# Building gate one-hots from bf16 comparisons of eight tokens, with most lookups on VectorE

## The chip, the cores and the metric

The kernel runs on one core of a Trainium2 chip. The metric is the device time of one execution in microseconds (us). Engines are named as in the profile: PE is TensorE's matmul, PEld its weight load, DVE VectorE, ACT ScalarE, POOL GpSimd, SP SyncE, which issues most transfers. SBUF is the memory on the core, PSUM the accumulators behind PE.

## The reference

One layer of an encoder for 1024 tokens of width 1024. The first half mixes tokens (a causal convolution beside an RWKV-7 recurrence). The second half, PEER, is where the change lies: each token picks, for each of 8 heads, 16 of 128 x 128 = 16384 experts by two lists of 128 keys.

```python
v1, i1 = lax.top_k(s1, PEER_TOPK)          # 16 best of 128 first keys, per head
v2, i2 = lax.top_k(s2, PEER_TOPK)          # 16 best of 128 second keys
cand = (v1[..., :, None] + v2[..., None, :]).reshape(..., 256)
sc, ci = lax.top_k(cand, PEER_TOPK)        # 16 best sums
experts = (jnp.take_along_axis(i1, ci // 16, -1) * 128
           + jnp.take_along_axis(i2, ci % 16, -1))
gates = jax.nn.softmax(sc, axis=-1)
...
z = einsum('td,tkd->tk', h, peer_u[experts])
y2 = einsum('tk,tkd->td', gelu(z) * gates, peer_v[experts])
```

Inputs and output are float32.

## The kernel before

The 1024 tokens are eight tiles of 128. Tiles 0 to 4 (`DT`) are computed densely: all 16384 experts are applied to them, each multiplied by a gate that is zero for experts that weren't picked. Tiles 5 to 7 (`GT`) gather their experts' rows by indirect DMA. The program has these stages:

- Up to about 1000 us: the input projection and the recurrence (chunks of 64 tokens). Between its matmuls run, as fill work, `front` (output projection, norms) and `query` (query projection, scores, top 16 of the keys) of token pairs 0 to 255, 256 to 511 and, later, 512 to 767.
- Then, without the recurrence: `front(768)`, `query(512)`, `query(768)`, with lookups (`choose`) stepped every `TSLOW` and gate matrices (`gate_matrix`) every `TGATE` steps, the latter at a higher priority for the planner. The planner orders the instructions of each engine by a simulated timeline; on the chip each engine then runs its list in order and waits on semaphores.
- From 1404 us: the dense loop over 32 groups of 4 x 128 experts, with the gathers of tiles 5 to 7 on POOL (indirect DMA) and DVE beside it.

`choose` handles one tile's lookups: top 16 of the 72 candidate sums (`best16`), then the position in each key list, then the key itself. That last step ("the lookup") is done for four heads in one pass, two passes for each of the two key lists: compare a small iota with the position (line 968, DVE, a one-hot `oh` in bf16), multiply by the keys (line 971), and sum over the 16 places. Line 971 and the sum run on the engine `E`: POOL for tiles 0 to 3, DVE for tiles 4 and 5 (`V if t0 >= LV`). On POOL the sum is a tree of additions that halve the one-hot (lines 977, 979); on DVE it is one reduction (line 974). The rows of keys and gates go to DRAM (`sel_d`); tiles 6 and 7 do the whole of it later, inside the dense loop, two heads at a time.

`gate_matrix` turns one dense tile's keys and gates into a 128 x 128 matrix per token, first key by second key. Keys and gates are loaded back and transposed by PE into PSUM (`selbank`; for tile 0 into a `mgate` bank), so that a column is a token. Then, for each four tokens (a group; 32 groups a tile, 160 in all): DVE compares the iota with the first keys into `oa` (line 1028) and with the second keys of three tokens into `ob` (line 1032); POOL multiplies these three by the gates (line 1034); ACT makes the fourth token's column from a square and a clamp (lines 1037, 1038); PE multiplies `ob` by `oa`, four matmuls in float32 (line 1040); ACT copies the product to `stage` (line 1041). Every 32 tokens a stage of 2 MB is written to `G_d` from ACT's queue (line 1048). The dense loop reads it back as `gmat`.

The tiles `oa` and `ob` have three buffers each, `stage` two and a third at times. Pages (`page`, a ring of `NPAGE` buffers of 2 KB) hold most of the other working tiles; `ident` and `iota` are constants.

Of the kernel before, what the change touches and what calls it, by code (L numbers as in the profile page):

```python
# [61 lines left out]
LV = 512  # L62
# [4 lines left out]
NPAGE = 31  # L67
# [3 lines left out]
GB = 3  # L71
# [14 lines left out]
def layer_kernel(ctx, tc, x, cols, c_row, cond_w, w_in, w2a2, g2, w_out, ln_rows, wq, keys, peer_u, peer_ut, peer_v, peer_vt, out):  # L86
# [17 lines left out]
    iota = const.tile([128, 128], F32)  # L104
    G.iota(iota, pattern=[[1, 128]], base=0, channel_multiplier=0, allow_small_or_imprecise_dtypes=True)
# [21 lines left out]
    sel_d = dt([3, 128, 128], "sel_d", 8)  # L127
    score_d = {t: [dram.tile([128, 512], F32, name=f"score_d{t}_{g}") for g in range(4)] for t in range(6, 8)}
# [23 lines left out]
    iota_q = const.tile([128, TOPK, TOPK], BF, name="iota_q")  # L152
    V.tensor_copy(iota_q, iota[:, :TOPK, None].to_broadcast([128, TOPK, TOPK]))
# [763 lines left out]
    def choose(tt, val, idx, h0, nh, nb, new, E):  # L917
# [21 lines left out]

        place = pos.bitcast(I32)  # L940
# [19 lines left out]
        put = lambda w, t: None if tt == DT[-1] else ld(sel_d[tt][w][:, h0 * TOPK:h0 * TOPK + n], t.rearrange("p h r -> p (h r)"))  # L960
        for half, sel in ((0, isel), (1, jsel)):
            ib = qb[:, 2 + half]
            A.activation(ib, idx[:, :, half, :], AF.Copy)
            for hh in range(0, nh, nb):
# [8 lines left out]
                if E is V:  # L973
                    V.tensor_reduce(fo[half][:, hs], oh.rearrange("p h q r -> p h r q"), axis=AX.X, op=OP.add)  # L974
                    continue
# [19 lines left out]
    def gate_matrix(tt, chosen):  # L995

        three = lambda nm: gb[0].tile([128, 3, 128], F32, name=nm)
        quad_ = lambda nm: gb[0].tile([128, 4, 128], F32, name=nm, bufs=GB)
        st = three("selt")
        if chosen:  # L1000
            s = [t.rearrange("p h r -> p (h r)") for t in chosen]
        else:
            kept_ = three("selr")
            s = [kept_[:, w] for w in range(3)]
            for w in range(3):
                ld(s[w], sel_d[tt][w])

        selbank.append(selbank.pop(0))
        pt = (selbank[0].tile([128, 512], F32, tag="mgate", name="selbank", bufs=1) if selbank[0] else mgate())[:, :384]
        pt = pt.rearrange("p (w t) -> p w t", w=3)  # L1010
        for w in range(3):
            T.transpose(pt[:, w], s[w], ident)
        A.activation(st, pt, AF.Copy)
        i1, i2, gt = (st[:, w] for w in range(3))
        if selbank[0]:
            i1, i2 = pt[:, 0], pt[:, 1]
        neg = three("selneg")
        A.activation(neg, pt, AF.Copy, scale=-1.0)
        for r0 in range(0, 128, TB):
# [5 lines left out]
            for q in range(0, TB, 4):  # L1025
                ts = slice(r0 + q, r0 + q + 4)
                oa, ob = quad_("oa"), quad_("ob")
# [344 lines left out]
```

## Time and profile before

| | |
|---|---|
| Time, median of 3 runs | 3225.45 us (3225.2 to 3225.85) |
| The profiled execution's own time | 3225.41 us, span 3223.5 us |
| PE busy | 2995.2 us (93%) |
| PEld busy | 2582.2 us (80%) |
| DVE busy | 2563.2 us (80%) |
| POOL busy | 1796.7 us (56%) |
| ACT busy | 1198.1 us (37%) |
| DMA | 922.30 MB, mean 286 GB/s |
| Mean granted TensorE clock | 0.953 |

Shares of the whole span are averages over stages with different limits, so the tables below give busy time by stretch. A row such as "L1028 DVE TENSOR_TENSOR oa<-iota,selbank" names the line in the kernel, the engine, the operation, and output and inputs by their tiles; buffer numbers are left out. "Idle before" is the time for which the engine waited ahead of the instruction, with what ended the wait.

### The profile page before, as it was taken

What the parts mean: (1) busy time and instruction counts of PE and PEld (TensorE: products, weight loads), DVE (VectorE), ACT (ScalarE), POOL (GpSimd) and SP (SyncE); (2) the same over time, 40 slices, a digit from 0 to 9 for tenths busy, and PEclk for the clock granted to TensorE, in tenths of its full rate; (3) what the DMA queues carried; (4) which work ended last, traced back from release to release, by engine and by line L of the source; (5) the groups of instructions that cost most, each with busy time, mean ns of one, the idle gap of its engine ahead of it and who ended that gap; (6) DMA issues with size and microseconds to landing.
All of it is one profiled execution on the core that took longest, in us unless ns stands there. A gap on an engine that the chain in (4) does not pass through costs nothing.

```text
span 3223.5 us, 53860 instructions
## 1 busy us (share of the span) xinstructions
PE 2995.2 (93%) x19952; PEld 2582.2 (80%) x19952; DVE 2563.2 (80%) x5612; ACT 1198.1 (37%) x2314; POOL 1796.7 (56%) x1408
## 2 busy tenths in 40 slices
PE   6968999899799589899999999999999999999995
PEld 4735677478688479899899988899989898999994
DVE  6279566856977979958999999898878777778788
ACT  5562344253353467552223232322323232222222
POOL 2410011133441853367777776787878777787872
PEclk9979899979699799999999999999999999999997
DMA  8876465378566898999999989899999999999994
GB/s 307 290 208 229 135 179 170 113 235 288 169 193 240 266 307 253 311 350 329 340 336 328 341 317 321 307 336 347 339 335 339 346 328 354 329 345 330 344 339 171
DMA packets 411782, 922.30 MB, mean 286 GB/s; under 512 B 81744, under 2 KB 221568, under 8 KB 389504
## 3 DMA queue, kind: packets, MB, share of 16 engines
q1 hardware_dynamic: 218688, 474.23, 43.2%
q0 software_dynamic: 110592, 402.70, 33.8%
q10 hardware_dynamic: 82240, 41.94, 4.6%
q8 instruction: 156, 2.56, 0.3%
q14 instruction: 106, 0.87, 0.1%
HBM read 788.91 MB, written 129.85 MB: 285 GB/s over the span
## 4 chain that ended last, share of the span: by engine, by line
PE 46%; DVE 13%; DMA 3%; issue 2%; ACT 1%; POOL 1%; SPq 0%; ACTq 0%; DVEq 0%; POOLq 0%
PE mg L1268 22%; PE md L1302 21%; DVE grow L1194 2%; PE mgate L1040 2%; DVE yacc L1307 1%; DVE gy L1201 1%; DMA vraw<-peer_vt 1%; PE mm L194 1%; DMA G_d<-stage 1%; DVE oa L1028 1%; DVE ob L1032 1%; DMA grow<-peer_v,eid 0%; DVE tkg L974 0%; DVE oh L968 0%; DVE bnst L202 0%
## 5 line engine op out<-in xcount | busy, mean ns | idle before, releaser
L1268 PE MATMUL mg<-h2h,uhi 128*128 128x320 f32 x2024 | 626.1, 309 | 8.0 <-DVE al L1274 8.0
L1268 PE MATMUL mg<-h2l,uhi 128*128 128x320 f32 x2024 | 625.1, 309 | 0.0
L1268 PE MATMUL mg<-h2h,ulo 128*128 128x320 f32 x2024 | 624.9, 309 | 0.0
L1201 DVE SCALAR_TENSOR_TENSOR gy<-grow,gz,gy 128x1024 f32<-128x1024 f32 x381 | 487.7, 1280 | 19.1 <-DMA grow<-peer_v,eid 17.3
L1302 PE MATMUL md<-vhi,al 128*128 128x512 f32 x1280 | 497.9, 390 | 0.0
L1302 PE MATMUL md<-vlo,ah 128*128 128x512 f32 x1280 | 496.5, 390 | 0.0
L1302 PE MATMUL md<-vhi,ah 128*128 128x512 f32 x1280 | 491.7, 391 | 4.1 <-DVE yacc L1307 2.1
L1194 DVE SCALAR_TENSOR_TENSOR grow<-grow,gh 128x1024 f32<-128x1024 f32 x384 | 460.6, 1210 | 25.6 <-DMA grow<-peer_u,eid 24.2
L1186 POOL DMA_INDIRECT grow<-peer_u,eid x384 | 363.1, 946 | 187.3 <-DVE grow L1194 78.4
L1186 POOL DMA_INDIRECT grow<-peer_v,eid x384 | 361.9, 942 | 187.6 <-DVE gy L1201 99.4
L1268 PEld LDWEIGHTS mg<-h2h,uhi 128*128 128x128 f32 x2024 | 379.9, 188 | 16.8 <-DVE al L1274 11.5
L1268 PEld LDWEIGHTS mg<-h2l,uhi 128*128 128x128 f32 x2024 | 379.9, 188 | 4.6
L1268 PEld LDWEIGHTS mg<-h2h,ulo 128*128 128x128 f32 x2024 | 379.9, 188 | 3.2
L1229 POOL TENSOR_TENSOR vlo<-vraw,vhi 128x1024 fp32r<-128x1024 f32 x128 | 309.0, 2414 | 32.4 <-ACT vhi L1227 30.0
L1229 POOL TENSOR_TENSOR ulo<-uraw,uhi 128x1024 fp32r<-128x1024 f32 x128 | 309.1, 2415 | 29.9 <-ACT uhi L1227 27.9
L1307 DVE TENSOR_TENSOR yacc<-md,yacc 128x512 f32<-128x512 f32 x310 | 210.6, 685 | 124.9 <-PE md L1302 124.3
L1302 PEld LDWEIGHTS md<-vhi,ah 128*128 128x128 f32 x1280 | 239.6, 188 | 53.1 <-ACT ah L1273 4.0
L1034 POOL TENSOR_TENSOR ob<-ob,selt 128x384 f32<-128x384 f32 x160 | 144.9, 907 | 241.7 <-DVE ob L1032 163.4
L1302 PEld LDWEIGHTS md<-vlo,ah 128*128 128x128 f32 x1280 | 240.3, 188 | 48.6
L1227 ACT ACTIVATE vhi<-vraw 128x1024 fp32r<-128x1024 f32 x128 | 135.2, 1056 | 387.8 <-DMA vraw<-peer_vt 369.9
L1302 PEld LDWEIGHTS md<-vhi,al 128*128 128x128 f32 x1280 | 240.3, 188 | 45.1 <-DVE al L1274 0.2
L182 POOL TENSOR_TENSOR wsplit<-wraw,wsplit 128x1024 fp32r<-128x1024 f32 x46 | 112.6, 2450 | 221.0 <-ACT wsplit L181 214.3
(404 smaller groups left out, 5916.8 us busy)
## 6 DMA issues: line engine op xcount, KB each, us to landing
uraw<-peer_ut SPq DMA_DIRECT2D x128, 512.0 KB, 7.1
vraw<-peer_vt SPq DMA_DIRECT2D x128, 512.0 KB, 5.5
wsplit<-split_wq SPq DMA_DIRECT2D x48, 1024.0 KB, 6.7
G_d<-stage ACTq DMA_DIRECT2D x20, 2048.0 KB, 13.6
gmat<-G_d SPq DMA_DIRECT2D x32, 1024.0 KB, 8.1
cw<-cond_w SPq DMA_DIRECT2D x48, 512.0 KB, 5.0
wsplit<-split_w_out SPq DMA_DIRECT2D x24, 1024.0 KB, 5.9
split_w_in<-wsplit SPq DMA_DIRECT2D x22, 1024.0 KB, 5.1
```

What stands on the lines that cost most here:

```text
L182: G.tensor_sub(lo, raw, hi.bitcast(F32))
L194: T.matmul(pt, l[:, k, :], r[k], start=i == 0, stop=i == 3 * KD - 1)
L1034: G.tensor_mul(ob[:, :3], ob[:, :3], gt[:, ts.start:ts.start + 3, None].to_broadcast([128, 3, 128]))
L1040: T.matmul(pt[:, t, :], ob[:, t, :], oa[:, t, :], start=True, stop=True)
L1186: G.indirect_dma_start(out=r, out_offset=None, in_=peer_u if k < 128 else peer_v, in_offset=bass.IndirectOffsetOnAxis(ap=eid[:, k % 128:k ...
L1194: V.scalar_tensor_tensor(r, r, 1.0, ht, op0=OP.mult, op1=OP.mult, accum_out=z[:, i:i + 1])
L1201: V.scalar_tensor_tensor(y, r, z[:, i - 128:i - 127], y, op0=OP.mult, op1=OP.add)
L1227: A.activation(hi, raw, AF.Copy)
L1229: G.tensor_sub(lo, raw, hi.bitcast(F32))
L1268: T.matmul(p, l[:, k, :], r[k][:, bs], start=i == 0, stop=i == 3 * KD - 1)
L1302: T.matmul(p, l[:, ts], r[:, e % 2, :], start=e == 0 and q == 0, stop=e == 3 and q == 2)
L1307: ins = V.tensor_add(ya, p, ya)
```

## The change

Gate one-hots: the keys of dense tiles are kept in bf16 (exact, since they are below 128) and transposed as bf16. For eight tokens at a time DVE compares a wide bf16 iota (`iota_e`, each value eight times) with the keys, once for each key list, into bf16 masks laid out key by token, three buffers. For each four tokens ACT copies the first mask to `oa` in float32, POOL multiplies three tokens of the second mask by the gates into `ob`, and DVE multiplies the fourth. The square and the clamp on ACT and the negated copy (`selneg`) are gone. `oa` has two buffers now, `ob` three.

Row loads: two transfers (bf16 keys from the new `keyb_d`, gates from `sel_d`) into a buffer of `ob`, in place of three into a buffer of their own.

Lookups: `LV` goes from 512 to 256, so that tiles 2 and 3 run line 971 and the sum on DVE; only the first pair (tiles 0 and 1) stays on POOL. Wherever all eight heads are done at once (tiles 0 to 5) the sum is the tree of additions, on either engine; the reduction stays for tiles 6 and 7.

Memory: `NPAGE` goes from 31 to 30. `iota` is no longer a constant: it is made once at the start for `iota_q`, and again in a page when the gate buffers are opened.

```diff
-LV = 512
+LV = 256
-NPAGE = 31
+NPAGE = 30
-GB = 3
+GB = 2, 3
+MB = 3
...
+    keyb_d = [dram.tile([2, 128, 128], BF, name=f"keyb_d{i}") for i in range(8)]
...
# choose
+        dense = tt in DT
...
+        if dense:
+            fo = qb[:, 4], qb[:, 5]
+        put = lambda w, t: None if tt == DT[-1] else ld((keyb_d if dense and w < 2 else sel_d)[tt][w][...], ...)
...
-                if E is V:
+                if nh < NH:
                     V.tensor_reduce(fo[half][:, hs], oh.rearrange("p h q r -> p h r q"), axis=AX.X, op=OP.add)
                     continue
                 for w in (8, 4, 2):
...
# gate_matrix
+            got = quad_("ob", GB[1]).rearrange("p t e -> p (t e)")
+            kb = got.bitcast(BF)[:, 0:256].rearrange("p (w k) -> p w k", w=2)
+            sg = got[:, 128:256]
+            ld(kb, keyb_d[tt].rearrange("w p k -> p w k"))
+            ld(sg, sel_d[tt][2])
...
-        for w in range(3):
-            T.transpose(pt[:, w], s[w], ident)
-        A.activation(st, pt, AF.Copy)
-        neg = three("selneg")
-        A.activation(neg, pt, AF.Copy, scale=-1.0)
+        keys_ = pt.bitcast(BF)[:, 0:256].rearrange("p (w k) -> p w k", w=2)
+        for w, k in enumerate((k1, k2)):
+            T.transpose(keys_[:, w], k, identb)
+        T.transpose(pt[:, 128:256], sg, ident)
+        gt = gb[0].tile([128, 128], F32, name="selt")
+        A.activation(gt, pt[:, 128:256], AF.Copy)
+        gv = pt[:, 128:256] if selbank[0] else gt
+        if not selbank[0]:
+            both = gb[0].tile([128, 2, 128], BF, name="selk2")
+            A.activation(both, keys_, AF.Copy)
+            keys_ = both
...
-                V.tensor_tensor(oa, iota[:, None, :].to_broadcast([128, 4, 128]),
-                                i1[:, ts, None].to_broadcast([128, 4, 128]), op=OP.is_equal)
-                V.tensor_tensor(ob[:, :3], iota[:, None, :].to_broadcast([128, 3, 128]),
-                                i2[:, ts.start:ts.start + 3, None].to_broadcast([128, 3, 128]), op=OP.is_equal)
-                G.tensor_mul(ob[:, :3], ob[:, :3], gt[:, ts.start:ts.start + 3, None].to_broadcast([128, 3, 128]))
-                A.activation(o, iota, AF.Square, bias=neg[:, 1, c])
-                A.activation(o, o, AF.Relu, bias=gt[:, c], scale=neg[:, 2, c])
+                if q % 8 == 0:
+                    masks = []
+                    for w in range(2):
+                        m = gb[0].tile([128, 128, 8], BF, name="mask", bufs=MB)
+                        V.tensor_tensor(m, iota_e, keys_[:, w, None, r0 + q:r0 + q + 8].to_broadcast([128, 128, 8]),
+                                        op=OP.is_equal)
+                        masks.append(m)
+                ma, mb = (m[:, :, q % 8:q % 8 + 4].rearrange("p e t -> p t e") for m in masks)
+                oa, ob = quad_("oa", GB[0]), quad_("ob", GB[1])
+                A.activation(oa, ma, AF.Copy)
+                c = r0 + q
+                G.tensor_mul(ob[:, :3], mb[:, :3], gt[:, c:c + 3, None].to_broadcast([128, 3, 128]))
+                V.tensor_mul(ob[:, 3], mb[:, 3], gv[:, c + 3:c + 4].to_broadcast([128, 128]))
```

More of the change, by code (lines that the diff above doesn't have):

```diff
@@ L152, in layer_kernel @@
     iota_q = const.tile([128, TOPK, TOPK], BF, name="iota_q")
+    iota = fe.tile([128, 128], F32, name="iota")
+    G.iota(iota, pattern=[[1, 128]], base=0, channel_multiplier=0, allow_small_or_imprecise_dtypes=True)
     V.tensor_copy(iota_q, iota[:, :TOPK, None].to_broadcast([128, TOPK, TOPK]))
@@ L959, in choose @@
         yield
-        put = lambda w, t: None if tt == DT[-1] else ld(sel_d[tt][w][:, h0 * TOPK:h0 * TOPK + n], t.rearrange("p h r -> p (h r)"))
+        if dense:
+            fo = qb[:, 4], qb[:, 5]
+        put = lambda w, t: None if tt == DT[-1] else ld((keyb_d if dense and w < 2 else sel_d)[tt][w][:, h0 * TOPK:h0 * TOPK + n],
+                                                        t.rearrange("p h r -> p (h r)"))
         for half, sel in ((0, isel), (1, jsel)):
@@ L995, in gate_matrix @@
     def gate_matrix(tt, chosen):
[L997 to L999 removed]
+        iota_e, identb = gb[1:]
+        quad_ = lambda nm, bufs: gb[0].tile([128, 4, 128], F32, name=nm, bufs=bufs)
         if chosen:
[L1001 removed]
+            k1, k2, sg = [t.rearrange("p h r -> p (h r)") for t in chosen]
         else:
[L1003 to L1018 removed]
+            got = quad_("ob", GB[1]).rearrange("p t e -> p (t e)")
+            kb = got.bitcast(BF)[:, 0:256].rearrange("p (w k) -> p w k", w=2)
+            sg = got[:, 128:256]
+            k1, k2 = kb[:, 0], kb[:, 1]
+            ld(kb, keyb_d[tt].rearrange("w p k -> p w k"))
+            ld(sg, sel_d[tt][2])
+        selbank.append(selbank.pop(0))
+        pt = selbank[0].tile([128, 512], F32, tag="mgate", name="selbank", bufs=1) if selbank[0] else mgate()
+        keys_ = pt.bitcast(BF)[:, 0:256].rearrange("p (w k) -> p w k", w=2)
[9 more added lines that the diff above has]
+            keys_ = both
         for r0 in range(0, 128, TB):
@@ L1067, in layer_kernel @@
             gb.append(fex.enter_context(tc.tile_pool(name="gb", bufs=1)))
+            iota = page("iota", w=128)
+            G.iota(iota, pattern=[[1, 128]], base=0, channel_multiplier=0, allow_small_or_imprecise_dtypes=True)
+            iota_e = gb[0].tile([128, 128, 8], BF, name="iota_e")
+            V.tensor_copy(iota_e, iota[:, :, None].to_broadcast([128, 128, 8]))
+            identb = gb[0].tile([128, 128], BF, name="identb")
+            V.tensor_copy(identb, ident)
+            gb.extend((iota_e, identb))
         if c < 14:
```

5 lines of the change are left out of this document (removed).

## The prediction

> **What bounds the kernel now.** I first read the busy time by stretch, cutting the span where the limiting engine changes. Each row gives length, then busy us and instruction count of PE, PEld, DVE, ACT and POOL, then granted clock, DMA share and GB/s.
>
> ```profile
> 860.00:1000.00 140.00, 131.91 (x1571) 117.89 (x1569) 117.11 (x342) 74.36 (x177) 57.83 (x59) 0.91 0.55 179
> ...
> 1055.00:1130.00 75.00, 43.08 (x201) 36.06 (x200) 72.47 (x174) 34.53 (x70) 66.31 (x66) 0.75 0.80 258
> 1130.00:1202.00 72.00, 56.50 (x421) 53.17 (x419) 58.01 (x163) 46.08 (x113) 37.98 (x39) 0.94 0.95 314
> 1202.00:1260.00 58.00, 57.71 (x481) 57.65 (x482) 50.42 (x222) 40.09 (x98) 19.25 (x24) 0.96 0.94 293
> 1260.00:1367.00 107.00, 92.27 (x751) 88.87 (x749) 106.59 (x318) 69.96 (x170) 40.24 (x40) 0.97 0.85 277
> 1367.00:1404.00 37.00, 34.90 (x264) 33.88 (x265) 21.49 (x39) 28.02 (x65) 18.86 (x22) 0.95 1.01 343
> 1404.00:3223.00 1819.00, 1771.31 (x9930) 1611.57 (x9928) 1516.71 (x2684) 516.23 (x848) 1342.92 (x1024) 0.99 0.91 328
> ```
>
> Gate matrices are built from 860 to 1404 us. After that comes the dense expert loop (1819 us, PE 1771 of them), which contains no changed line. So whatever the change is worth, it is worth it before 1404 us. Between 1055 and 1130 DVE is full (72.47 of 75) and PE half empty; the same from 1260 to 1367 (DVE 106.59 of 107, PE 92.27). From 1202 to 1260 and from 1367 on PE is full instead, and from 1130 to 1202 the DMA share is 0.95. The chain of waits, asked for each of those five stretches in turn, says the same:
>
> ```profile
> by line: DVE oa L1028 10.0%; DVE cand L932 9.0%; DVE ob L1032 8.2%; DVE oh L968 7.9%; DVE xt L837 7.1%; DVE rstd L212 5.1%; DVE bnst L202 4.8%; PE mm L819 4.0%; ACT xn L220 3.9%; DVE nbias L218 3.6%; issue 3.1%; DVE tkf L941 2.5%; DVE xt L8
> ...
> by line: DMA G_d<-stage 39.6%; DMA wsplit<-split_wq 12.7%; DMA selr<-sel_d 12.4%; DMA keys<-keys 7.2%; PE mgate L1040 5.5%; DVE xt L837 3.5%; ACT ob L1038 2.5%; ACT xt L220 2.0%; ACT stage L1041 1.7%; SPq L830 1.7%; DVE oa L1028 1.7%; SPq L
> ...
> by line: PE mm L194 52.3%; PE mgate L1040 38.7%; PE mm L891 8.5%; ACT ob L1038 0.9%; issue 0.1%
> ...
> by line: DVE oa L1028 13.6%; DVE tkg L974 12.2%; DVE ob L1032 11.5%; issue 8.7%; DVE oh L971 8.1%; DVE oh L968 5.5%; ACT stage L1041 3.8%; ACT ob L1037 2.7%; DVE h2lo L232 2.7%; DVE cand L781 2.3%; ACT ob L1038 2.1%; DVE tku L780 2.1%; DVE
> ...
> by line: PE mgate L1040 53.3%; PE md L1268 19.2%; PE mm L194 7.7%; PE mm L891 4.8%; ACT L1270 3.5%; PE mg L1268 2.8%; POOL ob L1034 2.3%; ACT stage L1041 2.1%; ACT ob L1038 2.1%; ACT ob L1037 1.9%; issue 1.3%; ACT md L1270 1.2%
> ```
>
> Look at the first item of each: DVE, DMA (the write of a finished gate block), PE, DVE, PE. A cheaper DVE instruction shortens the first and the fourth stretch only; in the others it is hidden by what their line names.
>
> **Gate one-hots.** The next fence is the view of the tiles oa, ob and stage: min/median/max ns of each instruction.
>
> ```profile
> L1028 DVE TENSOR_TENSOR oa<-iota,selbank x128: 630/675/690, 1003.8 to 1399.1; 128x512 f32<-128x512 f32 x128
> L1028 DVE TENSOR_TENSOR oa<-iota,selt x32: 647/693/2415, 864.1 to 994.1; 128x512 f32<-128x512 f32 x32
> ...
> L1037 ACT ACTIVATE ob<-iota,selneg x160: 383/393/444, 860.2 to 1400.3; 128x128 f32<-128x128 f32 x160
> L1038 ACT ACTIVATE ob<-ob,selt,selneg x160: 478/493/537, 861.1 to 1401.5; 128x128 f32<-128x128 f32 x160
> L1034 POOL TENSOR_TENSOR ob<-ob,selt x160: 818/827/2817, 867.4 to 1400.4; 128x384 f32<-128x384 f32 x160
> L1032 DVE TENSOR_TENSOR ob<-iota,selbank x128: 535/544/552, 1004.4 to 1399.7; 128x384 f32<-128x384 f32 x128
> ...
> L1041 ACT ACTIVATE stage<-mgate x160: 572/597/634, 875.9 to 1403.1; 128x512 f32<-128x512 f32 x160
> ...
> L977 POOL TENSOR_TENSOR oh<-oh x48: 420/868/1683, 835.2 to 1128.3; 128x512 bf16<-128x512 bf16 x16, 128x256 bf16<-128x256 bf16 x16, 128x128 bf16<-128x128 bf16 x16
> L968 DVE TENSOR_TENSOR oh<-iota_q,tkb x24: 677/684/2400, 824.1 to 1347.6; 128x1024 bf16<-128x1024 bf16 x24
> L971 POOL TENSOR_TENSOR oh<-oh,tkb x16: 1904/2214/4514, 824.9 to 1099.4; 128x1024 bf16<-128x1024 bf16 x16
> L979 POOL TENSOR_TENSOR tkg<-oh x16: 299/303/615, 845.8 to 1130.3; 128x64 f32<-128x64 bf16 x16
> L971 DVE TENSOR_TENSOR oh<-oh,tkb x8: 1209/1212/1843, 1308.6 to 1353.3; 128x1024 bf16<-128x1024 bf16 x8
> ...
> L968 DVE TENSOR_TENSOR loh<-iota_q,ltkb x16: 404/416/1252, 1540.9 to 2141.6; 128x512 bf16<-128x512 bf16 x16
> L971 DVE TENSOR_TENSOR loh<-loh,ltkb x16: 673/680/2301, 1541.8 to 2143.0; 128x512 bf16<-128x512 bf16 x16
> ...
> L983 DVE TENSOR_TENSOR tkg<-tkg,mx x6: 277/282/406, 819.5 to 1336.7; 128x128 f32<-128x128 f32 x6
> ```
>
> Now, per four tokens: DVE 0.675 + 0.544 = 1.219 us; ACT 0.393 + 0.493 for the fourth column and 0.597 for the stage copy, 1.48 us; POOL 0.827 us. After: half of two bf16 comparisons of 1024 elements each, that is one per four tokens. L968 is the same operation on the same size and type, with the iota laid out and a run of neighbours as the other operand: 0.684 us. Its small form (0.416 for 512) against L971 on DVE (0.680 for 512, 1.212 for 1024, where one operand stands still in the innermost dimension) shows that this form takes about half a nanosecond an element and the other a whole one. Here the innermost dimension is eight neighbouring tokens on both sides, as in L968. The one thing no row shows is a bf16 operand that lies in PSUM. Bounds: 0.684 (L968) and 1.212 (L971 on DVE). I take 0.684, since layout and type are those of L968, and L1028 costs no more from PSUM (0.675) than from SBUF (0.693).
>
> The Trainium skill does not agree with itself on this. Its page "VectorE: DVE Perf Modes", section "The perf-mode tier table", puts a two-tensor operation with any PSUM operand at one element a cycle; the section "Why PSUM operands drop a tier" on the same page allows the two-element mode for 16-bit data there. By the first the mask would cost as L971 does, and the time is that of the first rival below; by the second the sum stands. No run here shows a 16-bit PSUM operand yet.
>
> The fourth column on DVE is 128 elements; the nearest row is L983 (0.282). So DVE per four tokens: 0.684 + 0.282 = 0.966, a saving of 0.25 us. ACT swaps 0.886 us for one copy of 512 elements, bounded by the stage copy (0.597) and by the 0.886 it replaces; I take 0.6, so ACT falls to 1.2 us. It is no limit in any of the stretches (at most 70 of 107 us). POOL's product keeps its 384 elements: 0.827. The four matmuls keep their shapes. New waits: a mask (three buffers) waits for the ACT copies and POOL products of the pair before, and the fourth column for the matmuls three groups back; behind them on DVE stand the top-16 searches and lookups, and PE waits for those only through later tiles. Their likeness today is L1028's wait for the matmuls, 1.4 us in the first stretch and 0.2 us in the fourth (below); I take the same again.
>
> **Lookups.** DVE rows of 1055 to 1130, then POOL's; below them, for comparison, one DVE row of 1130 to 1202 and three of 1260 to 1367 (count | busy us, mean ns of one):
>
> ```profile
> L1028 DVE TENSOR_TENSOR oa<-iota,selbank 128x512 f32<-128x512 f32 x17 | 11.4, 670 | 1.4 <-PE mgate L1040 1.4
> L968 DVE TENSOR_TENSOR oh<-iota_q,tkb 128x1024 bf16<-128x1024 bf16 x6 | 10.6, 1827 | 0.0
> ...
> L932 DVE TENSOR_TENSOR cand<-vi 128x64 f32<-128x64 f32 (+2 forms) x8 | 7.1, 920 | 0.0
> L837 DVE TENSOR_TENSOR xt<-xt,row_g 128x512 f32<-128x512 f32 x4 | 5.9, 1530 | 0.0
> ...
> L218 DVE SCALAR_TENSOR_TENSOR nbias<-bnmv,rstd 128x1 f32<-128x1 f32 x4 | 4.2, 1062 | 0.0
> L212 DVE TENSOR_TENSOR rstd<-rstd,rnew 128x1 f32<-128x1 f32 x4 | 4.0, 1029 | 0.0
> ...
> L977 POOL TENSOR_TENSOR oh<-oh 128x512 bf16<-128x512 bf16 (+2 forms) x24 | 18.4, 788 | 0.0
> L971 POOL TENSOR_TENSOR oh<-oh,tkb 128x1024 bf16<-128x1024 bf16 x7 | 15.4, 2225 | 2.7 <-DVE oh L968 2.7
> ...
> L212 DVE TENSOR_TENSOR rstd<-rstd,rnew 128x1 f32<-128x1 f32 x4 | 0.5, 153 | 0.0
> ...
> L1028 DVE TENSOR_TENSOR oa<-iota,selbank 128x512 f32<-128x512 f32 x40 | 26.9, 672 | 0.3 <-PE mgate L1040 0.2
> ...
> L974 DVE TENSOR_REDUCE tkg<-oh 128x64 f32<-128x1024 bf16 x8 | 15.9, 2032 | 0.0
> ...
> L932 DVE TENSOR_TENSOR cand<-vi 128x64 f32<-128x64 f32 (+2 forms) x12 | 2.2, 218 | 0.0
> ```
>
> Tiles 2 and 3 (the second pair) move from POOL to DVE, and seven of their eight passes lie in the first stretch. Each took POOL 2.2 + 3 x 0.79 + 0.30 = 4.9 us. On DVE a pass is the product, 1.212 (L971 DVE), and four bf16 additions of 512, 256, 128 and 64 elements. The first is 0.416 (the 512 form of L968); 1024 against 512 gives 0.52 ns an element and 0.15 us fixed, so 0.28, 0.21 and 0.18 follow, together 1.1 us. That adds 8 x 2.3 = 18.5 us to DVE. Against it stands what POOL does to DVE in this stretch: L968 means 1.83 us where its median is 0.684, L932 0.92 where it is 0.218 later, L218 and L212 more than 1 us for one element a partition. The excess over 0.684, 0.218, 0.69 (L837, of L1028's size) and 0.15 (L212 in the next stretch) is 6 x 1.14 + 8 x 0.70 + 4 x 0.84 + 4 x 0.91 + 4 x 0.88 = 23 us in these lines alone. Of POOL's 66.31 busy us the lookups are 18.4 + 15.4 + 7 x 0.30 = 36, and they hold the longest single instructions, so I let 14 of the 23 us go. L1028 points the same way: with both operands in SBUF its maximum is 2415 ns, from PSUM 690.
>
> The Trainium skill has this rule: "SBUF — State Buffer", section "Who interferes with whom", says that a Vector instruction with two SBUF inputs competes with a GpSimd instruction that reads SBUF, and one with a single SBUF input does not. The trace agrees (2415 against 690). By that rule the new masks for tiles 1 to 4 stay clear of POOL, which the sum already has.
>
> First stretch: 17 groups x -0.25 = -4.3, +18.5, -14: **0 us**, with ends of -9 (all 23 us of excess gone) and +14 (none).
>
> Tiles 4 and 5 trade the reduction (8 x 2.03) for the same four additions (8 x 1.1): -7.3 us. With 40 groups x -0.25 = -10.2, the fourth stretch loses 17.5 us of DVE work. PE is the next limit there: 92.27 busy, so at most -14.7. Since two engines near nine tenths full never pack perfectly, I take **-12** (ends -5 and -14.7).
>
> 860 to 1000: 32 groups of tile 0, whose keys are copied to SBUF, so that they still compete with POOL; DVE 117 of 140, PE 131.91. DVE saves some 8 to 10 us, PE covers most: **-3** (ends -10 and 0).
>
> **Costed at nothing.** The other three stretches: PE and DMA cover them. Row loads: two per tile in place of three, into an ob buffer, so that SP waits for the matmuls of three groups before, with the split weights queued behind it. The old loads' waits on SP are the nearest row:
>
> ```profile
> L1006 SPq EVENT_SEMAPHORE  x8: 17/17/3754, 852.3 to 1114.3; - x8
> ```
>
> So at most four waits of 3.75 us, 15 us, and none if they behave as the median (17 ns); I take none, because weights are fetched three buffers ahead. If that cover goes, PE's projection (L194) waits. One page less (30): the nearest row is the late load of the keys, 7.2% of 72 us on the chain, so 0 to +5; I take 0. Building the wide iota once: about one L968, hidden in 860 to 1000. The second key row as bf16, the transposes and the dropped negation: fractions of a us per tile on PE and ACT, hidden by DVE.
>
> **Sum.** Made against the profiled execution, 3225.41 us (span 3223.5 and 1.9 around it); the median of the runs, 3225.45, is the same. -3 + 0 - 12 = -15: **3210 us**.
>
> **Rivals.**
> First, slower: the masks from PSUM go at one element a cycle, 1.212 us. Then a group costs 1.494 in place of 1.219, +0.275. First stretch 17 x 0.275 + 18.5 - 14 = +9.2, fourth 40 x 0.275 - 7.3 = +3.7, the start -3 (SBUF keys); from 1202 to 1260 DVE has 7.6 us of room under PE, enough for 27 groups at that price. Together +10: 3235. Of this sum 4.5 - 7.3 - 3 = -5.8 does not hang on the 57 groups, so it turns slower from +0.10 a group, a mask of 1.04 us. For it: no row shows the operand. Against: layout and type of L968. 0.16.
> Second, no change because the write of gate blocks takes over: DMA is at 0.85 in the fourth stretch and 1.01 behind it, and the second stretch already loses 39.6% of 72 us, 28 us, to one such write. If the 12 us come back as that wait, 3222 to 3225. Against: 0.85 x 107 leaves 16 us of room. 0.08.
> Third, no change because the matmuls' input now passes DVE, ACT and PE in line: oa came straight from DVE, and now waits in ACT's queue behind stage copies, where all that is queued behind a copy waits for its mask too. If one copy of 0.6 us is exposed per eight tokens, the 40 groups of the fourth stretch cost 20 x 0.6 = +12, which is its gain: 3222. Against: ACT gets 0.29 us a group emptier. 0.07.
> Fourth, no change because what stays on POOL (66.31 - 36 = 30 us in the first stretch) holds up the moved lookups as the lookups held up DVE: +14 - 12 - 3 = -1, 3224. Against: those instructions are shorter than a lookup's product. 0.07.
> The forecast keeps 0.62.
>
> **Numbers.** The forecast's own range adds its ends, -10 - 9 - 14.7 and 0 + 14 - 5: 3192 to 3234; ends seldom meet, so 3197 to 3222. To leave out no more than 2 in 10, the first rival and the loads' waits taken in, it is 3190 to 3235. About 0.2%, 6.5 us, is what can be told from no change: faster 0.62, same 0.20 (rivals two to four, less 0.02 for those that end further out), slower 0.18.
>
> **What would show it.** Masks near 0.68 us, mean, from PSUM; the fourth-column product near 0.28; the additions near 1.1 us a pass. The stretch with tiles 4 and 5's lookups about 12 us shorter and now PE-bound, L968 of tiles 2 and 3 nearer 0.7 than 1.8, and the dense loop starting at about 1389 instead of 1404 and taking its 1819 us. Wrong if the mask is over 1.04 us, if PE's idle time "until ACT oa" grows, or if the wait for the gate-block writes grows by what DVE saves.

## The result, and the profile after

The changed kernel takes 3245.0 us (median of 6 runs, 3235.7 to 3247.7) against 3224.9 for the kernel before on the same chip: ratio 1.0065, 95% interval 1.0046 to 1.0084. It is slower by 20 us where 15 us of gain were forecast, and outside the range of 3190 to 3235. The profiled execution took 3244.71 us (span 3242.9).

First the stretches of the forecast, from the view of busy time by stretch of the changed kernel (length, then PE, PEld, DVE, ACT, POOL, clock, DMA share, GB/s):

```profile
860.00:1000.00 140.00, 134.15 (x1543) 120.57 (x1544) 108.04 (x348) 80.48 (x140) 57.59 (x55) 0.90 0.55 175
1055.00:1130.00 75.00, 49.52 (x246) 40.99 (x247) 75.00 (x210) 43.95 (x61) 40.45 (x32) 0.84 0.82 273
1130.00:1202.00 72.00, 58.64 (x409) 54.31 (x408) 53.25 (x151) 57.73 (x91) 40.22 (x35) 0.91 0.91 292
1202.00:1260.00 58.00, 55.09 (x473) 54.22 (x471) 52.20 (x262) 43.30 (x67) 22.66 (x24) 1.00 0.97 322
1260.00:1367.00 107.00, 92.58 (x751) 89.75 (x751) 91.98 (x305) 72.51 (x115) 45.76 (x39) 0.97 0.77 253
1367.00:1404.00 37.00, 28.08 (x194) 25.80 (x192) 17.14 (x34) 31.51 (x42) 19.34 (x18) 0.91 0.96 316
1404.00:3242.90 1838.90, 1781.14 (x9962) 1620.14 (x9961) 1526.41 (x2687) 519.25 (x857) 1346.33 (x1026) 0.99 0.90 325
```

DVE has fallen as foreseen in the fourth stretch (91.98 us for 106.59), but PE has not moved up: 92.58 for 92.27. ACT rose where it should have fallen: 57.73 us for 46.08 between 1130 and 1202, and 31.51 of 37 behind 1367, where PE drops from 34.90 to 28.08. The view of the tiles says why (min/median/max ns):

```profile
L1044 ACT ACTIVATE oa<-mask x160: 1097/1148/1267, 855.5 to 1406.0; 128x512 f32<-128x512 bf16 x160
...
L1046 POOL TENSOR_TENSOR ob<-mask,selt x160: 986/1028/4182, 857.7 to 1406.0; 128x384 f32<-128x384 bf16 x160
L1047 DVE TENSOR_TENSOR ob<-mask,selbank x128: 320/379/407, 1005.6 to 1405.3; 128x128 f32<-128x128 bf16 x128
...
L1039 DVE TENSOR_TENSOR mask<-iota_e,selbank x128: 631/678/708, 1003.5 to 1404.2; 128x1024 bf16<-128x1024 bf16 x128
...
L1051 ACT ACTIVATE stage<-mgate x160: 569/597/702, 869.8 to 1408.5; 128x512 f32<-128x512 f32 x160
...
L983 DVE TENSOR_TENSOR oh<-oh x48: 206/308/1478, 1054.9 to 1342.8; 128x512 bf16<-128x512 bf16 x16, 128x256 bf16<-128x256 bf16 x16, 128x128 bf16<-128x128 bf16 x16
...
L977 DVE TENSOR_TENSOR oh<-oh,tkb x16: 1209/1218/2295, 1047.3 to 1332.0; 128x1024 bf16<-128x1024 bf16 x16
```

The masks from PSUM cost 0.678 us, as taken. Everything that reads a mask costs more than taken: the ACT copy `oa` 1.148 for 0.6, POOL's product 1.028 for 0.827, the fourth column 0.379 for 0.282. In a mask the experts of one token lie eight bf16 values, 16 bytes, apart. The last stage copy starts at 1408.5 us, 5 us later than before and not 15 earlier, and from there to the end it takes 14 us longer.

What PE waited for between 1055 and 1400, in the view of waits (us in total, times, longest): before,

```profile
PE mgate L1040 <- POOL ob L1034: 30.3, 17, 6.6
...
PE mgate L1040 <- ACT ob L1038: 11.5, 3, 7.2
```

and after:

```profile
PE mgate L1050 <- ACT oa L1044: 21.7, 22, 4.0
PE mgate L1050 <- POOL ob L1046: 16.5, 14, 3.6
PE mgate L1050 <- DVE ob L1047: 14.6, 9, 5.6
```

The gate matmuls waited 41.8 us for their inputs and now wait 52.8, 21.7 of it for ACT's copy (34.4 and 54.2 in a second profile of each kernel, used below). The same copy holds the other end: DVE waits for it before a new mask may overwrite an old one, in the same 345 us:

```profile
DVE mask L1039 <- ACT oa L1044: 10.5, 11, 1.9
```

And in the chain of waits from 1340 to 1410 (it reaches back to 1391 only), where PE's matmuls (L1040, L1268) led behind 1367 before, ACT's copy now leads:

```profile
by line: ACT oa L1044 9.3%; PE mgate L1050 4.9%; ACT stage L1051 4.5%; issue 2.7%; PE mg L1285 2.3%; POOL ob L1046 1.4%; DVE mask L1039 1.0%; ACTq L1058 0.5%; ACTq L1044 0.1%; POOLq L1046 0.1%
```

### The profile page after: what moved, and what is told of

Its sections match the earlier page's. It is cut to its first block, busy times and chain, and to the rows that moved or that the text cites. A ratio compares the mean times of both kernels' runs of the same rounds, so it can differ in the third digit from the quotient of the medians.

```text
span 3242.9 us, 53776 instructions
## 1 busy us (share of the span) xinstructions
PE 3012.1 (93%) x19952; PEld 2592.6 (80%) x19952; DVE 2562.9 (79%) x5678; ACT 1242.9 (38%) x2151; POOL 1800.7 (56%) x1369
## 4 chain that ended last, share of the span: by engine, by line
PE 37%; DVE 10%; DMA 4%; issue 3%; POOL 2%; ACT 1%; ACTq 0%; POOLq 0%; DVEq 0%
PE mg L1285 19%; PE md L1319 18%; DVE grow L1211 2%; DMA grow<-peer_v,eid 2%; DVE yacc L1324 1%; DVE gy L1218 1%; DMA grow<-peer_u,eid 1%; POOL grow L1203 1%; DMA vraw<-peer_vt 1%; POOL ulo L1246 1%; POOL vlo L1246 0%; DVE mg L1289 0%; DVE ltkg L980 0%; DVE loh L974 0%; DVE al L1291 0%
## 5 line engine op out<-in xcount | busy, mean ns | idle before, releaser
L1046 POOL TENSOR_TENSOR ob<-mask,selt 128x384 f32<-128x384 bf16 x160 | 176.7, 1118 | 247.1 <-DVE mask L1039 126.8
```

What stands on the lines that cost most here:

```text
L1046: G.tensor_mul(ob[:, :3], mb[:, :3], gt[:, c:c + 3, None].to_broadcast([128, 3, 128]))
```

## The experiments

Theory S: the copies and products read values 16 bytes apart and pay for it; in its place contiguous reads would give the forecast. Rival G: the moved lookups cost more than they bring. Rival O: the planner orders the dense loop by simulated times, so any edit ahead of it gives another order and another length. Diffs are against the changed kernel unless "before" is named.

**The reads by themselves.** Masks read contiguously; this mixes up the tokens of the one-hots, so only its time is meant.

```diff
-ma, mb = (m[:, :, q % 8:q % 8 + 4].rearrange("p e t -> p t e") for m in masks)
+ma, mb = (m.rearrange("p e t -> p (e t)")[:, 128 * (q % 8):128 * (q % 8) + 512]
+          .rearrange("p (t e) -> p t e", t=4) for m in masks)
```

> The changed kernel with the masks read as runs of neighbouring elements by ACT, POOL and DVE, where it reads every eighth element; the tokens of the one-hots are then mixed up, all else is the same work. Theory (the reads at a stride cost ACT 1.15 us for 0.6, POOL 1.03 for 0.83, DVE 0.38 for 0.28, and ACT's 1.75 us a group is what took the place of DVE): oa copy near 0.6 us, product on POOL near 0.83, last stage copy 8 to 20 us earlier than the changed kernel's 1408.5, so 1388 to 1400; the total then 3205 to 3237, as the dense loop's new order falls. Rival (a copy from bf16 to f32 costs ACT this whatever the stride): copy stays at 1.1 us and the last stage copy at 1404 to 1412. Second rival (the chain DVE, ACT, PE in line costs, not its length): copy at 0.6, last stage copy still later than 1402.

```profile
L1044 ACT ACTIVATE oa<-mask x160: 612/624/697, 856.7 to 1396.0; 128x512 f32<-128x512 bf16 x160
...
L1046 POOL TENSOR_TENSOR ob<-mask,selt x160: 821/828/5086, 858.8 to 1397.0; 128x384 f32<-128x384 bf16 x160
L1047 DVE TENSOR_TENSOR ob<-mask,selbank x128: 232/277/290, 1007.1 to 1394.7; 128x128 f32<-128x128 bf16 x128
```

3229.6 us, 1.0020 [1.0007, 1.0034]. All three durations are those of the forecast (0.624, 0.828, 0.277) and the last stage copy starts at 1399.2. The price of the distance is so 0.52 us on 512 elements for ACT, 0.20 on 384 for POOL and 0.10 on 128 for DVE. Of the 20 us, 15 are gone, but the forecast gain is not there. With the copy at its forecast price PE still waits for it, and longer than the changed kernel (4.1 us) for another result of ACT, `hf` (1055 to 1400):

```profile
PE mgate L1050 <- POOL ob L1046: 19.1, 10, 3.6
PE mgate L1050 <- ACT oa L1044: 15.8, 12, 7.1
PE mm L196 <- ACT hf L232: 15.7, 2, 13.7
```

The planner also made another order for this kernel: from 869 us on, DVE's instructions stand in another order than in the changed kernel. The 15 us are thus the worth of the reads and of that order together.

**The moved lookups.** `LV` back to 512 in the changed kernel; then `LV = 256` and the tree of additions for tiles 0 to 5 alone, on the gates of the kernel before.

```diff
-LV = 256
+LV = 512
```

```diff
# on the kernel before
-LV = 512
+LV = 256
...
-if E is V:
+if nh < NH:
```

> The changed kernel with tiles 2 and 3's lookups back on POOL (tiles 4 and 5 keep the additions on DVE). Theory: moving these lookups is worth about nothing in the gate stage, so last stage copy 1402 to 1415. Rival (the move to DVE made the first full-DVE stretch longer, and is the loss): last stage copy before 1402. The total varies with the dense loop's order, 3215 to 3250.

> The kernel before with the lookups of the change alone: tiles 2 and 3 on DVE, the tree of additions for tiles 4 and 5 on DVE. Gate one-hots as before. Theory by the prediction's own sum (first full-DVE stretch neutral without the one-hots' 4 us, so +4; fourth -7): last stage copy 1395 to 1405. Theory after e4_gates (the move takes 40 us of POOL work off a stretch where POOL was 88% busy): last stage copy 1380 to 1395. Rival: DVE, still at 1.22 us a group, pays for all of it: 1408 to 1420. Dense part 1818 to 1838.

Without the move 3263.1 us, 1.0117 [1.0098, 1.0136], last stage at 1436.6: in the changed kernel the move is worth 28 us of the gate stage by one profile of each, and 18 us of the time, where the forecast had nothing net. The first stretch of the kernel with lookups on POOL:

```profile
1055.00:1130.00 75.00, 34.08 (x148) 28.80 (x147) 57.57 (x150) 32.67 (x46) 64.43 (x60) 0.70 0.65 220
```

PE does 34.08 us of work there, against 49.52 with the lookups on DVE; POOL is busy 64.43 for 40.45, and DVE, which lost work, does less rather than being freed. On the old gates the move brings the last stage to 1384.3, and the time to 3221.4, 0.9997 [0.9977, 1.0017]: no gain at the end. Rival G falls; where the gain went is the question of rival O.

**The dense order.** Both kernels with a barrier ahead of the dense loop and a planner without its time model, so that the dense instructions stand in one and the same order in both; then one and three POOL memsets ahead of the first gather, which change the dense order alone.

```diff
+    tc.strict_bb_all_engine_barrier()
     pg2x.close()
...
-    with tile.TileContext(nc, schedule_with_timeline_sim=True) as tc:
+    with tile.TileContext(nc) as tc:
```

```diff
         pend = []
+        if t == GT[0]:
+            for _ in range(n):      # n = 1 (before), 3 (changed)
+                G.memset(grow(), 0.0)
```

> The kernel before, planned without the simulated timeline (program order and priorities alone) and with a barrier of all engines ahead of the dense loop, so that the dense loop's instruction order does not depend on what stands ahead of it. It is the base for the next run. Both theories: slower than the kernel before, 3260 to 3400 us, since the dense loop's first loads lose their head start. Its dense part (from the last stage copy to the end) is the number to compare with the next run's.

> The changed kernel in the same dress; the dense loop then has the same instruction order on every engine as in e1_plain_before. Theory (of the 20 us, some 14 come from the order that the planner made anew in the dense loop, 5 from the gate stage): dense part within 3 us of e1_plain_before, gate stage 0 to 10 us later. Rival (the change itself makes the dense loop slower, by where tiles lie or by what it leaves behind): dense part longer by 10 us or more here too.

> The kernel before with one more instruction, a POOL memset of a gather row ahead of the first gather. It takes about 1 us and stands behind the gate stage, which keeps its order on every engine; but the planner then orders the dense loop anew. Theory (the dense loop's length depends on the order that the planner happens to make): gate stage as before (last stage copy 1402 to 1405), dense part changed by more than 1 us, anywhere from -6 to +15 us against 1820. Rival (orders are worth the same): dense part within 2 us of 1820.

> The changed kernel with three such memsets (with one its order stayed): gate stage in the same order, the dense loop in a new one. Theory: last stage copy 1407 to 1410 as in the changed kernel, dense part different from its 1834 by more than 3 us, 1818 to 1838. Rival (the longer dense loop belongs to the change): dense part stays at 1831 to 1837, plus up to 3 us for the memsets.

Plain, the kernels take 3779.0 and 3765.0 us, 1.1723 [1.1702, 1.1745] and 1.1670 [1.1639, 1.1701] of before: far over the 3260 to 3400 that were expected; the change is 14 us faster, by intervals that just part. Its last stage starts at 1501.3 against 1511.4, 10 us earlier where 0 to 10 later was expected, and the rest takes 2265.7 against 2262.2. With the dense order fixed, the dense part is within 3.5 us of the same, though at 2262 us it is another part than the one of 1820. So in another order of the gate stage the change, with the same reads, brings no loss. With the time model, the nudged kernel before has its last stage at 1397.5, 1831.5 us behind it in a profiled execution of 3231.4 us, and a median of 3226.9, 1.0014 [0.9998, 1.0031]; the nudged changed kernel 3245.4, 1.0066 [1.0040, 1.0092]. So with another order the dense part of before is as long as that of after, while its time hardly moves, and the changed kernel stays 20 us up in either order: rival O loses ground.

**Both kernels again.** A second profile of each.

> The kernel before unchanged, a second profile. Theory A, the dense length belongs to the planned order: from the last stage copy to the end 1820 us again, within 3, and the last stage at 1403 within 3. Theory B, the dense length swings from one execution to the next like the time does (the kernel has been seen from 3208 to 3235): 1825 to 1835 is as likely as 1820.

> The changed kernel unchanged, a second profile. Theory A (dense length belongs to the order): 1834 again within 3 and the last stage at 1408.5 within 3. Theory B (it swings with the execution): the dense part between 1824 and 1840, and the gate stage's end may move by several us as well.

```profile
L1041 ACT ACTIVATE stage<-mgate x160: 572/597/631, 869.2 to 1389.2; 128x512 f32<-128x512 f32 x160
```

```profile
L1051 ACT ACTIVATE stage<-mgate x160: 569/597/686, 869.9 to 1405.5; 128x512 f32<-128x512 f32 x160
```

The kernel before, instruction for instruction the same, now has its last stage at 1389.2 in place of 1403.1, and ends within 3 us of where it did (3222.5). The changed one repeats: 1405.5, 3243.9. The forecast's "1389 instead of 1404" is a step that the kernel before takes by itself.

Counting the dense matmuls (lines 1268 and 1302 before) in each trace places the loss. From the end of the last stage copy to the 400th of them it is 59 to 61 us in the profiles of the planner with time model (64 and 66 in two with a page less), and from the 5000th to the last 885 to 887 in all of them. What differs lies between the 400th and the 5000th. That stretch, in the view of busy time, for the kernel before, for it again, and after (length, PE, PEld, DVE, ACT, POOL, clock, DMA share, GB/s):

```profile
1464.00:2301.00 837.00, 824.93 (x4605) 746.90 (x4604) 755.59 (x1591) 243.63 (x399) 628.89 (x479) 1.00 0.92 331
```

```profile
1450.00:2298.00 848.00, 830.59 (x4606) 751.28 (x4605) 757.75 (x1594) 242.71 (x400) 630.62 (x480) 0.99 0.91 327
```

```profile
1470.00:2320.00 850.00, 829.65 (x4601) 750.84 (x4600) 762.51 (x1592) 242.41 (x400) 631.81 (x482) 0.99 0.92 327
```

The same 4600 matmuls keep PE busy for 824.93, 830.59 and 829.65 us, and it idles for the rest, 12, 17 and 20 us. The column of the clock reads 1.00, 0.99, 0.99. The trace's record of the granted clock has it at 0.5 for 3.4 us, or twice that, behind some of PE's idle gaps in this stretch: never in the first profile of before, 5.1 us lost in the second and after. The Trainium skill, "TensorE: Matmul & The Clock Gate", section "Part 1: The HAM clock gate", says that the clock is halved after an idle window of some 3.4 us and, with one busy core, knows only these two values. The records agree on the values and on the length of a step (in the dense part 0.5 for 3.413 or 6.827 us at a time), but not on the idle time: the longest idle gaps of PE in the 5 us ahead of the three steps in the changed kernel are 2.0, 3.8 and 2.5 us, so a gap shorter than 3.4 us was enough for two of them, while one of 2.3 us drew no step. In the first profile of before the longest gap of this stretch is 1.9 us. Taking idle and lost clock away leaves 822.0 to 826.0 us in all eighteen profiles made with the planner's time model; the table gives ten:

| kernel | last stage starts | 400th to 5000th | PE idle | lost to the clock |
|---|---|---|---|---|
| before, and again | 1403.1, 1389.2 | 837, 847 | 12, 17 | 0, 5 |
| before, nudged | 1397.5 | 850 | 19 | 5 |
| before, lookups moved | 1384.3 | 853 | 22 | 7 |
| after, and again | 1408.5, 1405.5 | 850, 852 | 20, 22 | 5, 7 |
| after, nudged | 1409.0 | 849 | 20 | 3 |
| after, contiguous reads | 1399.2 | 845 | 17 | 5 |
| after, compact pairs (below) | 1383.5 | 845 | 16 | 5 |
| before, 30 pages (below) | 1401.3 | 859 | 24 | 10 |

So the dense part is no constant: up to the 5000th matmul DVE is 90% busy (755.59 of 837) with late lookups and gathers, PE waits for it now and then, and pays again in clock. PE's largest wait in total in the 900 us behind the last stage copy, before:

```profile
PE mg L1268 <- DVE al L1274: 8.0, 9, 1.9
```

and after:

```profile
PE mg L1285 <- DVE al L1291: 14.9, 12, 3.8
```

**Another layout.** Pairs of tokens, 4 bytes apart, for the first mask only, compared with a view of the wide iota; then for both masks with a compact iota of two copies.

```diff
-m = gb[0].tile([128, 128, 8], BF, name="mask", bufs=MB)
+m = gb[0].tile([128, 4, 128, 2], BF, name="mask", bufs=MB)
...
-iota_e = gb[0].tile([128, 128, 8], BF, name="iota_e")
+iota_e = gb[0].tile([128, 128, 2], BF, name="iota_e")
```

> The changed kernel with the first mask laid out in pairs of tokens, so that ACT's copy into oa reads every second bf16 element (4 bytes apart) where it read every eighth (16 bytes apart). Results as before. Theory (the price of a read grows with the distance): oa copy 0.6 to 0.9 us, mask still 0.68, last stage copy 1399 to 1407. Rival (any distance but one costs the same): copy at 1.1 to 1.2 us, last stage copy 1406 to 1412. Second rival: the mask loses its rate with runs of two, 1.2 us, and the last stage copy comes after 1412. Dense part 1818 to 1838.

> The changed kernel with both masks stored in pairs of tokens, four bytes apart, and compared with a compact iota of two copies (512 contiguous bytes per partition) in place of the one of eight copies; the product on POOL is split in two instructions, two tokens and one. The pair mask compared with a strided iota took 1.089 us against 0.678. Theory A, the strided iota lost the rate: with the compact one the masks return to about 0.68 us, the copy on ACT stays at 0.62, the product on VectorE comes to about 0.28, and the copy of the last stage starts near 1399 to 1402 as with contiguous reads. Theory B, the keys' runs of two lost it: masks stay near 1.09 us, VectorE gains 2 x 0.41 less about 2 x 0.1 a pair of groups, some 0.3 us a group, and the last stage comes at about 1414 or later. Total by A about 3228 to 3235, by B 3250 to 3260, the dense part between 1823 and 1840 in either.

With a view of the wide iota:

```profile
L1051 ACT ACTIVATE oa<-mask x160: 613/623/657, 856.8 to 1411.9; 128x512 f32<-128x512 bf16 x160
...
L1045 DVE TENSOR_TENSOR mask<-iota_e,selbank x64: 1046/1089/1140, 1010.8 to 1409.1; 128x1024 bf16<-128x1024 bf16 x64
L1040 DVE TENSOR_TENSOR mask<-iota_e,selbank x64: 636/677/706, 1011.8 to 1410.1; 128x1024 bf16<-128x1024 bf16 x64
```

and with the compact one:

```profile
L1044 ACT ACTIVATE oa<-mask x160: 614/623/697, 853.9 to 1381.6; 128x512 f32<-128x512 bf16 x160
...
L1046 POOL TENSOR_TENSOR ob<-mask,selt x160: 603/614/2041, 856.6 to 1381.0; 128x256 f32<-128x256 bf16 x160
L1047 POOL TENSOR_TENSOR ob<-mask,selt x160: 390/400/2612, 857.7 to 1381.6; 128x128 f32<-128x128 bf16 x160
L1039 DVE TENSOR_TENSOR mask<-iota_e,selbank x128: 658/679/693, 998.3 to 1379.2; 128x1024 bf16<-128x1024 bf16 x128
L1048 DVE TENSOR_TENSOR ob<-mask,selbank x128: 228/279/292, 1001.1 to 1380.9; 128x128 f32<-128x128 bf16 x128
```

Read 4 bytes apart, the copy is back at 0.623. But pairs of the wide iota, 16 bytes from pair to pair, cost the comparison its rate (1.089 for 0.677), and that kernel took 3254.6, 1.0085 [1.0056, 1.0115], its last stage at 1414.2, as the second rival had it. DVE, ACT and POOL run their instructions in the very order of the changed kernel there (PE too, but for ten matmuls of the recurrence at 541 us), so this pair of kernels holds the order fixed: the copy is 0.52 us cheaper every four tokens, one mask is 0.41 dearer every eight, and the time is no shorter (3254.6 for 3245.0, with intervals that overlap). PE waits less for the copy (1055 to 1400) but more for POOL's product, whose own reads are still 16 bytes apart:

```profile
PE mgate L1057 <- POOL ob L1053: 34.1, 16, 4.8
PE mgate L1057 <- ACT oa L1051: 10.0, 7, 3.0
```

So at this order the copy's price alone does not set the end of the gate stage.

With the compact iota the mask is 0.679 with the same pairs of keys, so the distance of the iota did it. POOL's product, split in two, costs 0.614 + 0.400, nearly the 1.028 of the changed kernel. The last stage of this kernel starts at 1383.5, and its PE waited less for the gates' inputs, and more for `hf`:

```profile
PE mgate L1051 <- ACT oa L1044: 14.2, 14, 3.0
PE mm L196 <- ACT hf L232: 12.5, 2, 10.5
PE mgate L1051 <- POOL ob L1046: 9.7, 9, 2.1
...
PE mgate L1051 <- POOL ob L1047: 2.6, 2, 1.9
PE mgate L1051 <- DVE ob L1048: 0.8, 1, 0.8
```

The gates' inputs come to 27.3 us for 52.8. It takes 3221.8 us, 1.0001 [0.9988, 1.0014]: by the ratios to before this layout, with the order that the planner made for it, is worth 21 us, all that the change lost, and no more than that. Two other dense orders of it:

> The changed kernel with compact pair masks and one memset of POOL ahead of the first gather: gate order kept, another dense order. Theory A (the order sets some 10 us of the dense part): the last stage stays at about 1385, the time lands anywhere from 3212 to 3238. Theory B (the dense part is fixed by what enters it): 3222 again within 4 us.

> The same with three memsets. Theory A: anywhere from 3212 to 3238; theory B: 3222 to 3226, the memsets being 2.9 us of POOL at most.

3223.6, 1.0012 [0.9994, 1.0030], and 3220.1, 0.9994 [0.9979, 1.0010]. The three agree within 4 us, and their last stages start at 1383.5, 1385.1 and 1392.5. With the two orders of the changed kernel within 0.4 us of each other, and those of before within 5, rival O falls: the dense order swings the time by a few us, not by 20.

**The page.** The kernel before with one page less, then with ten and twelve memsets (as above) ahead of the first gather, for other dense orders.

```diff
-NPAGE = 31
+NPAGE = 30
```

> The kernel before with 30 pages in place of 31, and nothing else. Theory (the prediction costed the page at nothing): the last stage starts within 5 us of 1403 and the time is within 0.5% of before. Rival, the missing page delays the early stretches: the last stage starts 8 us or more later with the same gate instructions. The dense order may be planned anew, so the dense part may come out anywhere from 1820 to 1840.

> The kernel before with 30 pages and ten memsets of POOL (0.95 us each, scratch rows) ahead of its first gather: the order up to the dense part is kept, the dense order is another. Theory A, the order set the price of the page kernel: the time returns to within 0.5% of before, with 837 to 850 us from the 400th to the 5000th dense matmul in place of 859. Theory B, the page itself costs it: again 3240 to 3255. The memsets lie where POOL has nothing to do yet and should cost 0 to 4 us.

> The same with twelve memsets, a third dense order. Theory A: between 3215 and 3245, not the same as the first by more than the noise; theory B: 3240 to 3255 again.

3248.8 us, 1.0095 [1.0074, 1.0117]; 3242.9, 1.0067 [1.0041, 1.0092]; 3247.6, 1.0081 [1.0055, 1.0107]. A page less costs the kernel before at least as much as the whole change did, in three dense orders. The gate stage is not late (1401.3, 1399.3 and 1401.3); the stretch of the dense matmuls, 853 and 854 us in the last two, is in the first:

```profile
1462.00:2321.00 859.00, 834.98 (x4602) 755.14 (x4601) 776.04 (x1593) 243.35 (x400) 630.67 (x480) 0.99 0.90 322
```

24 us of idle and 834.98 busy, 10 of them lost to a halved clock. The changed kernel has 30 pages too, and so has the compact one, which shows no such loss. The last two runs gave the compact kernel its page back, the second in another dense order (one memset):

```diff
-NPAGE = 30
+NPAGE = 31
...
-both = gb[0].tile([128, 2, 128], BF, name="selk2")
+both = quad_("ob", GB[1]).rearrange("p t e -> p (t e)").bitcast(BF)[:, 0:256]
+       .rearrange("p (w k) -> p w k", w=2)
```

> The changed kernel with compact pair masks and the 31st page given back (the copied keys of the first tile live in a buffer of ob, which has then two left for that tile). Theory A, the missing page costs some 20 us whatever the gates are: 3195 to 3208, with the last stage earlier than 1385 or fewer than 845 us from the 400th to the 5000th dense matmul. Theory B, the page's loss belongs to the plans of the kernel before: 3215 to 3230, as with 30 pages. The buffer taken from ob may cost the first tile up to 3 us, in a stretch that the recurrence bounds.

> The same with one memset of POOL ahead of the first gather, for another dense order. Theory A: within 8 us of the first and below 3212; theory B: 3215 to 3230.

3220.7, 0.9998 [0.9988, 1.0008], and 3222.5, 1.0004 [0.9992, 1.0015]: the page is worth nothing there. In the first the last stage starts at 1398.0, 14.5 us later than with 30 pages, and the rest is 7.6 us shorter (1824.7 for 1832.3); the profiled execution, of 3225.4 us, was among the longer ones. No version was faster than the kernel before by more than the noise.

## Why the prediction was wrong

**The step that failed first: the price of reading the new layout, above all "one copy of 512 elements ... I take 0.6".** The copy measured 1.148, above the upper end (0.886) as well. Neither row behind the bounds reads bf16 values 16 bytes apart; the bounds were of the right operation at the wrong layout. With it "ACT falls to 1.2 us" became 1.148 + 0.597 = 1.75, up from 1.48. The other two readers were taken at the price of contiguous values too: POOL's product at 0.827 for a measured 1.028, the fourth column at 0.282 for 0.379, so that DVE saves 0.16 us every four tokens and not 0.25. The forecast also called ACT no limit, "at most 70 of 107 us", and overlooked its own row of 1367 to 1404, 28.02 of 37, which is a larger share; there the copy took the lead. The contiguous kernel (15 us less by the ratios) and the compact one (21 less) differ from the changed kernel in this layout and in the order that the planner made for it. The Trainium skill has a rule that speaks against the change and that the prediction did not weigh: "SBUF — State Buffer", section "Door 1: The DMA port swizzle", says that reads are at full rate as long as at least two in a row fall into one line of 16 bytes. The runs agree for the copies: 16 bytes apart 1.148, 4 bytes apart 0.623, contiguous 0.624.

**The third rival's mechanism, at .07, is seen**: `oa` waits in ACT's queue, and "PE's idle time until ACT oa" grew to 21.7 us, as the last paragraph of the forecast listed. Its price was set with a 0.6 us copy, 12 us. With such a copy 15.8 us of this wait are left in the contiguous kernel and 14.2 in the compact one, each in its own order, so most of it does not hang on the long copy. That the compact kernel then took 3221.8, the rival's 3222, is luck: its gate stage was not late, as the rival would have it.

**"First stretch ... 0 us."** Off by much in the changed kernel, where the move is worth 28 us of the gate stage and 18 of the time; on the old gates it is worth 12 us of the gate stage against the mean of three profiles of before (1396.6), and nothing in the time. The relief was taken as 14 of 23 us of excess in named lines; of these L974 (L968 before) fell from 1.83 to 1.03 us, the one-element L220 (L218) from 1.06 to 0.24, and 22 groups of masks passed in the stretch where 17 did:

```profile
L1039 DVE TENSOR_TENSOR mask<-iota_e,selbank 128x1024 bf16<-128x1024 bf16 x22 | 14.6, 673 | 0.0
...
L839 DVE TENSOR_TENSOR xt<-xt,row_g 128x512 f32<-128x512 f32 x4 | 4.4, 1146 | 0.0
...
L974 DVE TENSOR_TENSOR oh<-iota_q,tkb 128x1024 bf16<-128x1024 bf16 x4 | 3.9, 1027 | 0.0
...
L220 DVE SCALAR_TENSOR_TENSOR nbias<-bnmv,rstd 128x1 f32<-128x1 f32 x4 | 0.9, 238 | 0.0
```

This gain paid for part of what the dearer reads cost, so the two errors were of opposite sign.

**"The dense loop, which contains no changed line ... worth before 1404 us."** Its instructions are unchanged, but its length went from 1820 to 1834 us, and the profile of before was the shortest of all (no half-clock step). A gate stage that ends earlier is not kept: lookups alone end it 19 us earlier than the profiled before and gain nothing, 10 us going to PE idle and 7 to the clock between the 400th and the 5000th matmul. The second profile of before shows the same exchange with no edit at all. This step fails even where the reads have their forecast price: the compact kernel's last stages, 1383.5 to 1392.5, are where the forecast had them (1389), and its time is 3220 to 3224, not 3210.

**"One page less ... I take 0."** In the kernel before it costs 0.67 to 0.95%, 22 to 31 us, far over the bound of 5. In the compact kernel it costs nothing. It can't be added to the sum either way.

**Right**: the masks at 0.678 us from PSUM, so the first rival, whose 3235 came nearest to the time, was refuted by its own condition. Of the two sections of the Trainium skill's "VectorE: DVE Perf Modes" that the prediction set against each other, "Why PSUM operands drop a tier" is borne out. Right too: DVE's work in the fourth stretch fell by 14.6 us, near the 17.5 foreseen; PE had no use for it.

**What the 20 us are.** With means over the profiles: last stage 1407.7 in the three of the changed kernel's gates and 1396.6 in the three of before (with the nudge), +11; the 400th to the 5000th matmul 850.4 and 844.6, +6; together 17 of the 20. The three of the changed gates lie within 3.5 us, those of before within 14. Every version with cheaper reads ends its gate stage earlier than all three of the changed kernel, 1399.2 contiguous, 1383.5 to 1392.5 compact, 1398.0 and 1398.5 compact with 31 pages, and this in three planned orders of that stage. So the layout makes the loss in this kernel, by the durations and the planned order together; how much is due to either is not shown. In the changed kernel's own order a cheap copy with one dear mask ended later still (1414.2), and without the time model the same dear reads ended 10 us earlier than before. Nor are ACT's copy and DVE's fourth column told apart; POOL's product is not needed for the gain, as the compact kernel has it at 1.014. That the second part, +6, belongs to the change is not shown: it lies within what two executions of one kernel differ by (837 and 847).

**Open**: what the reads cost at a fixed order. Why 30 pages lengthen the dense part of the kernel before, when pages are closed by then and three dense orders agree. The stages ahead of it are planned anew with a page less; that was not held fixed, and the changed kernel itself was not run with 31 pages. Also open is what of the dense part's idle time could be had by an order made for it.

## What to carry to other kernels

Before a producer's layout is changed for its own speed, price each reader at the new distance between its elements: here the comparison became twice as fast an element while the copy behind it took twice as long, and a layout in pairs kept both prices low. Profile the kernel before twice, and take the sum over boundaries that don't trade with each other: here the end of one stage moved by 14 us and the next gave it back. Where a planner orders by simulated time, time a part of the change in more than one order (here other orders of the dense loop moved the time by a few us), and see whether two versions stand in the same order before their difference is put down to the edit.

## What the runs showed of the hardware

- Reading bf16 at 16 bytes apart: ACT 1148 ns for 624 (512 elements), POOL 1028 for 828 (384), DVE 379 for 277 (128). At 4 bytes apart ACT took 623: no price.
- A comparison of bf16 on DVE keeps its rate with one operand in PSUM (1024 elements in 678 ns, and 693 with both in SBUF) and with runs of two (679), but not when the runs of two of one operand lie 16 bytes apart (1089). By the rule of the Trainium skill named above two values in each line of 16 bytes are read at full rate; this comparison was not.
- PE's granted clock falls to half for 3.4 us steps even in a part that is 97% busy on PE: five such dips, one of them twice as long, 10 us lost, in the dense part of before with 30 pages, and none in the first profile of before with the same matmuls. In the changed kernel idle gaps of 2.0 and 2.5 us were enough for a dip, and one of 2.3 us was not.
